# Paired heads in three attention stages of a fused block: score row halves side by side, values as the stationary operand in column halves, weights normalised before they are transposed

## The chip, the cores and the metric

One core of a Trainium2 chip runs the whole kernel. The metric is device time in microseconds (us). TensorE (PE) multiplies matrices; its weight loads are listed apart as PEld. VectorE is DVE, ScalarE is ACT, GpSimd is POOL, SyncE is SP. A matmul whose operands are plain float32 is issued as two instructions, one whose operands are float32r (the rounded high or low half of a split) as one.

## The reference

The reference is two transformer layers followed by a second block, on 512 tokens of width 1024. Three of its parts matter here.

- `swa_sinks`: 16 query heads of width 64 over 4 key heads. Query block n of 128 tokens sees key blocks n-1 and n, masked to a window of 128; a per-head sink joins the softmax.

```
s = einsum('bnqkgd,bnskd->bnkgqs', q, kb) * 64 ** -0.5        # banded: [128, 256] a block
p = softmax(concatenate([where(valid, s, -1e30), sink], -1))[..., :-1]
o = einsum('bnkgqs,bnskd->bnqkgd', p, vb)
```

- `stick_breaking_attention`: 8 heads of width 64 over all earlier keys.

```
z = einsum('bhqd,bhkd->bhqk', qb, k) * scale
log_one_minus = where(strict, log_sigmoid(-z), 0)
suffix = cumsum(log_one_minus, reverse) - log_one_minus
w = where(strict, exp(log_sigmoid(z) + suffix), 0);  o = w @ v
```

- `latent_attention`: 8 heads, keys of width 96, values of width 64, causal softmax.

## The kernel before

Tiles are 128 partitions by up to 512 columns. Weights arrive by DMA, are split by ACT and DVE into float32r halves (`weights`, lines 146 to 155), and every dense product is three float32r matmuls (`mm3` and `mmhl`, lines 157 to 166). The program is emitted in source order, and the framework's scheduler then orders each engine's instructions; each engine executes its own list strictly in that order.

**Banded stage** (`attention`, lines 1291 to 1500). Work goes by head pairs t = 0 to 7; a pair's two heads r sit in partitions 0 to 63 and 64 to 127 of the query tile `q`/`qhl` and of the key tile `kf`/`khl`. `proj(t)` makes the queries (24 matmuls `psq`). `scores(t)` (line 1383) writes score tiles `sc` in PSUM, head by head, three matmuls of 64 rows a block (line 1401; one float32 matmul for block 0, line 1397), and DVE masks each block and takes its row maximum (line 1402). `expo(t)` takes exponentials on ACT with their sums (line 1418), adds the sink and takes the reciprocal `den` on DVE (lines 1420, 1421). `mixed(t)` transposes the weights 128 by 128 into `pt` (line 1433), copies them out as `pT`, multiplies with `pT` stationary and the 64 value columns moving into `po` (line 1443), scales by `den` on DVE (line 1446) and transposes the result back (`pto`, line 1450). The loop over t weaves `scores(t-1)`, `proj(t)`, `mixed(t-2)` and `expo(t-1)`.

**Stick-breaking stage** (`second`, lines 1752 to 1790). Per head, `part1` makes the logits `z` (four float32 matmuls of 64 rows, line 1756, each followed by a mask matmul with `idr`, line 1757), then absolute value, exponential and logarithm on ACT, then three DVE passes (lines 1764 to 1766) for the halves `hl`. `part2` adds the triangular sums into `z` (20 matmuls, line 1774), takes the exponential (line 1776) and multiplies with the values stationary into 64 columns (line 1780). The loop keeps one head in flight: `part1(h)`, then `part2(h-1)`.

**Latent stage** (lines 1795 to 1921). `scores(h)` (line 1864), then `mixed(h)` a head later: exponentials, transposes (line 1880), copies `pT`, products with `pT` stationary into `po` (line 1887); after each second head one scaling by `den` (line 1916), four transposes `pto` (line 1919) and one copy `ob` (line 1920).

**Filler.** `fill(n)` (line 1661) issues n steps of the gate projection, three float32r matmuls `psg` of 512 columns each; 192 steps in all, and `fill(1000)` at the end of the latent stage issues what is left.

Of the kernel before, what the change touches and what calls it, by code (L numbers as in the profile page):

```python
# [1290 lines left out]
def attention(N, kvd, rd, gpost, after_half):  # L1291
# [3 lines left out]
    with ExitStack() as es:  # L1295
# [4 lines left out]
        with ExitStack() as e2:  # L1300
# [82 lines left out]
            def scores(t):  # L1383
                a = t // 4
                q, qhl = qs.pop(t)
                S = [[N.mp.tile([P, 2 * W], F32, tag="m", name="S") for _ in range(2)] for _ in range(4)]
                m = qp.tile([P, 4, 2], F32, tag="m", name="m")
                for j in range(4):
                    r = j % 2
                    rows = slice(64 * r, 64 * r + 64)  # L1390
                    ps = scp.tile([P, 2, 2 * W], F32, tag="sc", name="sc")
                    for n in (j - r, j - r + 1):
                        s0 = W if n == 0 else 0
                        qb = slice(n * W, (n + 1) * W)
                        pn = ps[:, n % 2, :]
                        if n == 0:
                            nc.tensor.matmul(pn[:, W:], lhsT=q[rows, qb], rhs=kf[rows, a, 0:W], start=True, stop=True, skip_group_check=True)
                        else:
                            kb = slice((n - 1) * W, (n + 1) * W)
                            for x, y, st, sp in ((0, 0, n == 2, False), (0, 1, False, False), (1, 0, False, True)):  # L1400
                                nc.tensor.matmul(pn, lhsT=qhl[rows, x, qb], rhs=khl[a][rows, y, kb], start=st, stop=sp, skip_group_check=True)
                        nc.vector.tensor_tensor_reduce(out=S[n][r][:, s0:], in0=pn[:, s0:], in1=mask[:, s0:], scale=1.0, scalar=-3e38, op0=ALU.add, op1=ALU.max, accum_out=m[:, n, r:r + 1])
                    yield
                sk = N.rows[:, None, 256 + 2 * t:258 + 2 * t].to_broadcast([P, 4, 2])
                nc.vector.tensor_tensor(out=m, in0=m, in1=sk, op=ALU.max)
                es_ = qp.tile([P, 4, 2], F32, tag="es", name="es")
                nc.vector.tensor_tensor(out=es_, in0=sk, in1=m, op=ALU.subtract)
                nc.vector.tensor_scalar(out=m, in0=m, scalar1=-1.0, scalar2=None, op0=ALU.mult)
                nc.scalar.activation(out=es_, in_=es_, func=AF.Exp)
                Ss[t] = S, m, es_  # L1410

            def expo(t):
# [6 lines left out]
                    yield  # L1419
                nc.vector.tensor_tensor(out=den, in0=den, in1=es_, op=ALU.add)  # L1420
                nc.vector.reciprocal(out=den, in_=den)
                Ss[t] = S, den

            def mixed(t):
                a = t // 4
                S, den = Ss.pop(t)
                po = N.mm.tile([P, 4, 2, 64], F32, tag="mm", name="po")
                for n in range(4):
                    s0 = W if n == 0 else 0
                    pt = scp.tile([P, 2, 2 * W], F32, tag="sc", name="pt")  # L1430
# [9 lines left out]
                    for r in range(2):  # L1440
                        d0 = (2 * a + r) * 64
                        for sb in range(s0 // W, 2):
                            nc.tensor.matmul(po[:, n, r, :], lhsT=pT[:, r, sb * W:(sb + 1) * W], rhs=v[:, n - 1 + sb, d0:d0 + 64], start=n == 0 and r == 0, stop=sb == 1, skip_group_check=True)  # L1443
                    yield
                ot = qp.tile([P, 4, 2, 64], F32, tag="ot", name="ot")
                nc.vector.tensor_tensor(out=ot, in0=po, in1=den[:, :, :, None].to_broadcast([P, 4, 2, 64]), op=ALU.mult)
                yield
                pt = N.mm.tile([P, T], F32, tag="mm", name="pto")
                for n in range(4):
# [160 lines left out]
def second(N, out, angd, hs):  # L1610
# [116 lines left out]
    with ExitStack() as e1:  # L1727
# [21 lines left out]

            return t[:, BASE[i] + P * max(0, q0 - i):BASE[i] + P * (4 - i)]  # L1750

        def part1(h):
            a, rows = h // 2, slice(64 * (h % 2), 64 * (h % 2) + 64)
            z = zp.tile([P, 1536], F32, tag="z", name="z")
            for i in range(4):
                nc.tensor.matmul(seg(z, i), lhsT=sk_[a][rows, i * P:(i + 1) * P], rhs=sq_[a][rows, i * P:], start=i < 3, stop=False, skip_group_check=True)  # L1756
                nc.tensor.matmul(z[:, BASE[i]:BASE[i] + P], lhsT=idr, rhs=msk, start=False, stop=False, skip_group_check=True)
# [9 lines left out]
            return z, hl, e  # L1767

        def part2(h, z, hl, w):
            rows = slice(64 * (h % 2), 64 * (h % 2) + 64)  # L1770
# [4 lines left out]
            fill(6)  # L1775
            nc.scalar.activation(out=w, in_=z[:, 0:1280], func=AF.Exp)
            fill(4)
            pv = N.mm.tile([P, T], F32, tag="mm", name="pv")
            for i in range(4):
                nc.tensor.matmul(pv[rows, i * P:], lhsT=sv[:, i, 64 * h:64 * h + 64], rhs=seg(w, i), start=i == 0, stop=i == 3, skip_group_check=True, tile_position=(0, 64 * (h % 2)))  # L1780
            nc.scalar.activation(out=oa[rows, h // 2, :], in_=pv[rows], func=AF.Copy)

        prev = None
        for h in range(9):
            cur = part1(h) if h < 8 else None
            fill(4)
# [9 lines left out]
    with ExitStack() as e1:  # L1796
# [71 lines left out]
                fill(1)  # L1868
            return S, mx

        def mixed(h, S, mx, po):
            sc = 96.0 ** -0.5
            r = h % 2
            nc.vector.tensor_scalar(out=mx, in0=mx, scalar1=-sc, scalar2=None, op0=ALU.mult)
            for i in range(4):
                nc.scalar.activation(out=S[i], in_=S[i], func=AF.Exp, scale=sc, bias=mx[:, i:i + 1], accum_out=den[:, i, r:r + 1])
                pt = ptp.tile([P, T], F32, tag="pt", name="pt")
                n = P * (i + 1)
                for sb in range(i + 1):
                    nc.tensor.transpose(pt[:, sb * P:(sb + 1) * P], S[i][:, sb * P:(sb + 1) * P], N.ident)  # L1880
                pT = tp.tile([P, T], F32, tag="pT", name="pT")
                if i % 2:
                    nc.vector.tensor_copy(pT[:, :n], pt[:, :n])
                else:
                    nc.scalar.activation(out=pT[:, :n], in_=pt[:, :n], func=AF.Copy)
                for sb in range(i + 1):
                    nc.tensor.matmul(po[:, i, r, :], lhsT=pT[:, sb * P:(sb + 1) * P], rhs=v[:, sb, 64 * h:64 * h + 64], start=i == 0 and r == 0 and sb == 0, stop=sb == i, skip_group_check=True)
                fill(1)

        heads(0)  # L1890
        wv = N.weights(N.ins["w_ukv"][1])
# [10 lines left out]
        for h in range(9):  # L1902
            if h < 8:
                if h % 2 == 0 and h < 6:
                    heads(h // 2 + 1)
                cur = scores(h)
            if prev is not None:
                g = h - 1
                if g % 2 == 0:
                    po = N.mm.tile([P, 4, 2, 64], F32, tag="mm", name="po")  # L1910
                    den = tp.tile([P, 4, 2], F32, tag="den", name="den")
                mixed(g, *prev, po)
                if g % 2:
                    nc.vector.reciprocal(out=den, in_=den)
                    ot = tp.tile([P, 4, 2, 64], F32, tag="x", name="ot", bufs=1)
                    nc.vector.tensor_tensor(out=ot, in0=po, in1=den[:, :, :, None].to_broadcast([P, 4, 2, 64]), op=ALU.mult)
                    pt = ptp.tile([P, T], F32, tag="pt", name="pto")
                    for n in range(4):
                        nc.tensor.transpose(pt[:, n * P:(n + 1) * P], ot[:, n].rearrange("p r d -> p (r d)"), N.ident)
                    nc.scalar.activation(out=ob[:, g // 2, :], in_=pt, func=AF.Copy)  # L1920
            prev = cur
    fill(1000)
    N.mmctx.close()
# [127 lines left out]
```

## Time and profile before

| what | us |
|---|---|
| median of 3 runs | 2767.73 (2764.96 to 2768.2) |
| the profiled execution, its own time | 2768.43 |
| span of that execution | 2766.7 |
| PE busy | 2680.9 (97% of the span) |
| PEld busy | 2330.6 (84%) |
| DVE busy | 1477.9 (53%) |
| ACT busy | 1167.9 (42%) |
| POOL busy | 27.4 (1%) |

The profile page gives shares over the whole span; the three stages of the change lie at 1716 to 1843 us (banded), 2369.8 to 2531 us (stick-breaking) and 2563 to 2664 us (latent). In a timeline the stretch of a merged row runs from its first start to its last end, and ends of matmuls are modelled, so the pace of PE is read from starts: (stretch - one duration) / (count - 1).

### The profile page before, as it was taken

The page shows a single profiled execution, that of the slowest core. Times are in us where ns is not written, and L with a number is a line of the kernel's source. Part 1 is how long each engine was busy: PE and PEld are TensorE (multiplying, and loading weights), DVE is VectorE, ACT ScalarE, POOL GpSimd, SP SyncE. Part 2 cuts the span into 40 slices and gives each one's busy share as a digit, 9 for nine tenths or more (in the row PEclk, how much of TensorE's full clock was granted, in tenths as well). Part 3 has the DMA queues.
Part 4 walks back from the last instruction along what each step waited for, and adds up shares of the span by engine and source line. Part 5 has one row for each costly group of instructions (what it writes and reads, how often), then busy time and mean ns, then how long its engine had stood idle before and what let it go on. Part 6 is the DMA issues. An engine that isn't in the chain of part 4 may idle for free.

```text
span 2766.7 us, 43687 instructions
## 1 busy us (share of the span) xinstructions
PE 2680.9 (97%) x17470; PEld 2330.6 (84%) x17470; DVE 1477.9 (53%) x2976; ACT 1167.9 (42%) x2072; POOL 27.4 (1%) x52
## 2 busy tenths in 40 slices
PE   8999988999999999999999999999999999999998
PEld 7888887788788999999888888888888898777877
DVE  8724466555557565467643447547424465234555
ACT  5223325345355554345432324445323335454643
POOL 0000000000000000000000000000000000000000
PEclk9999999999999999999999999899999999999999
DMA  6622316864765463245342323012222323113333
GB/s 212 218 94 98 115 63 203 238 174 129 214 209 142 133 215 109 96 138 180 115 133 92 99 92 141 25 38 93 98 94 97 114 85 115 61 61 105 115 126 99
DMA packets 207556, 344.20 MB, mean 124 GB/s; under 512 B 66164, under 2 KB 136180, under 8 KB 207352
## 3 DMA queue, kind: packets, MB, share of 16 engines
q1 hardware_dynamic: 206920, 341.13, 39.0%
q8 instruction: 137, 2.24, 0.3%
q14 instruction: 67, 0.55, 0.1%
q10 hardware_dynamic: 432, 0.28, 0.0%
HBM read 298.51 MB, written 41.26 MB: 123 GB/s over the span
## 4 chain that ended last, share of the span: by engine, by line
PE 88%; DVE 4%; DMA 3%; ACT 3%; issue 1%; SPq 0%; DVEq 0%; ACTq 0%
PE gu L165 11%; PE gu L164 11%; PE gu L166 11%; PE o L164 8%; PE o L166 8%; PE o L165 8%; PE ps L594 4%; PE ps L166 2%; PE ps L165 2%; PE ps L164 2%; PE psg L164 2%; PE psg L165 1%; PE psg L166 1%; PE po L1443 1%; PE z L1756 1%
## 5 line engine op out<-in xcount | busy, mean ns | idle before, releaser
L153 ACT ACTIVATE whl<-wr 128x1024 fp32r<-128x1024 f32 x417 | 439.3, 1059 | 729.3 <-PE gu L166 402.1
L154 DVE TENSOR_TENSOR whl<-wr,whl 128x1024 fp32r<-128x1024 f32 x417 | 508.1, 1222 | 374.1 <-ACT whl L153 373.0
L164 PE MATMUL gu<-xn,whl 128*128 128x512 f32 (+1 forms) x1200 | 436.7, 366 | 8.9 <-ACT xn L242 7.1
L165 PE MATMUL gu<-xn,whl 128*128 128x512 f32 (+1 forms) x1200 | 439.2, 366 | 3.9 <-DVE xn L243 3.9
L166 PE MATMUL gu<-xn,whl 128*128 128x512 f32 (+1 forms) x1200 | 438.0, 366 | 0.8 <-DVE whl L154 0.8
L166 PE MATMUL o<-a,whl 128*128 128x256 f32 (+1 forms) x906 | 297.7, 329 | 0.0
L165 PE MATMUL o<-a,whl 128*128 128x256 f32 (+1 forms) x906 | 296.8, 329 | 0.0
L164 PE MATMUL o<-a,whl 128*128 128x256 f32 (+1 forms) x906 | 296.3, 329 | 0.0
L164 PEld LDWEIGHTS gu<-xn,whl 128*128 128x128 f32 x1200 | 226.6, 190 | 45.1 <-ACT xn L242 7.3
L165 PEld LDWEIGHTS gu<-xn,whl 128*128 128x128 f32 x1200 | 228.0, 190 | 40.8 <-DVE xn L243 5.2
L166 PEld LDWEIGHTS gu<-xn,whl 128*128 128x128 f32 x1200 | 228.0, 190 | 37.0 <-DVE whl L154 1.2
L165 PE MATMUL gu<-pair,whl 128*128 128x256 f32 x704 | 200.2, 285 | 1.1 <-DVE pair L243 1.1
L166 PE MATMUL gu<-pair,whl 128*128 128x256 f32 x704 | 199.1, 283 | 1.2 <-DVE whl L154 1.2
L164 PE MATMUL gu<-pair,whl 128*128 128x256 f32 x704 | 199.2, 284 | 0.0
L165 PEld LDWEIGHTS o<-a,whl 128*128 128x128 f32 x906 | 170.7, 189 | 17.1
L166 PEld LDWEIGHTS o<-a,whl 128*128 128x128 f32 x906 | 170.6, 189 | 17.0
L164 PEld LDWEIGHTS o<-a,whl 128*128 128x128 f32 x906 | 170.3, 189 | 17.1
L594 PE MATMUL ps<-mxe,wraw 128*128 128x256 f32 x544 | 144.4, 416 | 15.2 <-DVE mxe L609 7.5
L594 PEld LDWEIGHTS ps<-mxe,wraw 128*128 128x128 f32 x544 | 108.9, 208 | 38.1 <-DVE mxe L609 7.7
L166 PEld LDWEIGHTS gu<-pair,whl 128*128 128x128 f32 x704 | 133.6, 190 | 2.0 <-DVE whl L154 1.4
L165 PEld LDWEIGHTS gu<-pair,whl 128*128 128x128 f32 x704 | 133.2, 189 | 2.4 <-DVE pair L243 1.7
L164 PEld LDWEIGHTS gu<-pair,whl 128*128 128x128 f32 x704 | 132.8, 189 | 1.0
(440 smaller groups left out, 4768.5 us busy)
## 6 DMA issues: line engine op xcount, KB each, us to landing
wr<-in_ffn_w_in_dram SPq DMA_DIRECT2D x204, 512.0 KB, 3.5
wr<-in_ffn_w_out_dram SPq DMA_DIRECT2D x99, 512.0 KB, 3.4
wr<-in_w_in_dram SPq DMA_DIRECT2D x38, 512.0 KB, 3.5
wraw<-in_w_rkvo_dram SPq DMA_DIRECT2D x32, 512.0 KB, 4.1
wr<-in_w_rkvo_dram SPq DMA_DIRECT2D x32, 512.0 KB, 4.6
wr<-in_w_ada_dram SPq DMA_DIRECT2D x24, 512.0 KB, 4.1
wr<-in_w_qo_dram SPq DMA_DIRECT2D x16, 512.0 KB, 3.4
gates<-xf SPq DMA_DIRECT2D x48, 128.0 KB, 1.8
```

The costliest lines, as they stand in the source:

```text
L153: nc.scalar.activation(out=hl[:, 0, :cols], in_=raw[:, :cols], func=AF.Copy)
L154: nc.vector.tensor_tensor(out=hl[:, 1, :cols], in0=raw[:, :cols], in1=hl[:, 0, :cols].bitcast(F32), op=ALU.subtract)
L164: nc.tensor.matmul(ps, lhsT=wh, rhs=xh, start=start, stop=False, **k)
L165: nc.tensor.matmul(ps, lhsT=wh, rhs=xl, start=False, stop=False, **k)
L166: nc.tensor.matmul(ps, lhsT=wl, rhs=xh, start=False, stop=stop, **k)
L594: nc.tensor.matmul(ps, lhsT=w[:, b * P:(b + 1) * P], rhs=x, start=start, stop=stop)
L1443: nc.tensor.matmul(po[:, n, r, :], lhsT=pT[:, r, sb * W:(sb + 1) * W], rhs=v[:, n - 1 + sb, d0:d0 + 64], start=n == 0 and r == 0, stop=sb ...
L1756: nc.tensor.matmul(seg(z, i), lhsT=sk_[a][rows, i * P:(i + 1) * P], rhs=sq_[a][rows, i * P:], start=i < 3, stop=False, skip_group_check=True)
```

## The change

Banded stage: `scores` now emits the two heads of a pair alternately, matmul by matmul. `expo` is followed by eight `tensor_scalar` instructions on POOL that multiply the exponentials by `den` in place. `mixed` makes the 64 value columns the stationary operand, writes head r to partitions 64r to 64r+63 of `po` (`tile_position=(0, 64 * r)`), alternates the heads, and splits `po` directly: the scaling on DVE and the four transposes `pto` are gone.

Stick-breaking stage: heads go by pairs. `products` emits the logits of both heads alternately and then all mask matmuls; `logs` is the ACT and DVE chain of one head; `weigh` the triangular sums and the exponential; `mixed` alternates the two heads' column halves of one `pv` tile. The loop runs over pairs, with 18 fill steps in each.

Latent stage: `weigh` normalises on POOL (four instructions a head) and copies the transposes into a layout by key block; `mixed` multiplies a pair at once, values stationary, column halves alternating; the scaling, the `pto` transposes and two of the float32 tiles are gone.

```diff
             def scores(t):
...
-                for j in range(4):
-                    r = j % 2
-                    for n in (j - r, j - r + 1):
-                            for x, y, st, sp in ((0, 0, n == 2, False), (0, 1, False, False), (1, 0, False, True)):
-                                nc.tensor.matmul(pn, lhsT=qhl[rows, x, qb], rhs=khl[a][rows, y, kb], start=st, stop=sp, skip_group_check=True)
+                for n2 in range(0, 4, 2):
+                    pss = [scp.tile([P, 2, 2 * W], F32, tag="sc", name="sc") for _ in range(2)]
+                    for n in (n2, n2 + 1):
+                        for x, y, st, sp in ((0, 0, n == 2, False), (0, 1, False, False), (1, 0, False, True)) if n else ((None, None, True, True),):
+                            for r in range(2):
+                                if n:
+                                    nc.tensor.matmul(pn, lhsT=qhl[rows, x, qb], rhs=khl[a][rows, y, kb], start=st, stop=sp, skip_group_check=True)
...
-                Ss[t] = S, den
+                for n in range(4):
+                    for r in range(2):
+                        nc.gpsimd.tensor_scalar(out=S[n][r][:, s0:], in0=S[n][r][:, s0:], scalar1=den[:, n, r:r + 1], scalar2=None, op0=ALU.mult)
+                Ss[t] = S
             def mixed(t):
...
-                            nc.tensor.matmul(po[:, n, r, :], lhsT=pT[:, r, sb * W:(sb + 1) * W], rhs=v[:, n - 1 + sb, d0:d0 + 64], start=n == 0 and r == 0, stop=sb == 1, skip_group_check=True)
+                    for sb in range(s0 // W, 2):
+                        for r in range(2):
+                            nc.tensor.matmul(po[64 * r:64 * r + 64, n * W:(n + 1) * W], lhsT=v[:, n - 1 + sb, d0:d0 + 64], rhs=pT[:, r, sb * W:(sb + 1) * W], start=n == 0, stop=sb == 1, skip_group_check=True, tile_position=(0, 64 * r))
-                nc.vector.tensor_tensor(out=ot, in0=po, in1=den[:, :, :, None].to_broadcast([P, 4, 2, 64]), op=ALU.mult)
-                    nc.tensor.transpose(pt[:, n * W:(n + 1) * W], ot[:, n].rearrange("p r d -> p (r d)"), N.ident)
-                N.split(pt, o, 0, T)
+                N.split(po, o, 0, T)
...
+        def products(a):
+            zs = [zp.tile([P, 1536], F32, tag="z", name="z") for _ in range(2)]
             for i in range(4):
+                for r, z in enumerate(zs):
+                    nc.tensor.matmul(seg(z, i), lhsT=sk_[a][rows, i * P:(i + 1) * P], rhs=sq_[a][rows, i * P:], start=i < 3, stop=False, skip_group_check=True)
+            for z in zs:
+                for i in range(4):
+                    nc.tensor.matmul(z[:, BASE[i]:BASE[i] + P], lhsT=idr, rhs=msk, start=False, stop=False, skip_group_check=True)
...
-        for h in range(9):
-            cur = part1(h) if h < 8 else None
-            fill(4)
-            if prev is not None:
-                part2(h - 1, *prev)
-            prev = cur
+        zs, ws = products(0), None
+        for a in range(4):
+            if ws:
+                mixed(a - 1, ws)
+            hls, ws = zip(*(logs(z) for z in zs))
+            fill(10)
+            weigh(zs[0], hls[0], ws[0])
+            fill(5)
+            weigh(zs[1], hls[1], ws[1])
+            fill(3)
+            if a < 3:
+                zs = products(a + 1)
+        fill(2)
+        mixed(3, ws)
...
+        def weigh(S, mx, pT):
+                nc.vector.reciprocal(out=den[:, i:i + 1], in_=den[:, i:i + 1])
+                nc.gpsimd.tensor_scalar(out=S[i], in0=S[i], scalar1=den[:, i:i + 1], scalar2=None, op0=ALU.mult)
...
+        def mixed(a, pTs):
+            po = N.mm.tile([P, T], F32, tag="mm", name="po")
+            for sb in range(4):
+                for r, pT in enumerate(pTs):
+                    nc.tensor.matmul(po[64 * r:64 * r + 64, sb * P:], lhsT=v[:, sb, 64 * h:64 * h + 64], rhs=pT[:, sb, sb:].rearrange("p i q -> p (i q)"), start=sb == 0, stop=sb == 3, skip_group_check=True, tile_position=(0, 64 * r))
+            nc.scalar.activation(out=ob[:, a, :], in_=po, func=AF.Copy)
```

The scheduler does not keep the alternation everywhere. Engine PE, banded stage, the scores of the second head pair; two `sc` tiles with consecutive numbers are the two heads of one block pair, so a row with a count is one head on its own. Before:

```order
L1397 MATMUL sc_16833<-kf_16343,q0_16803 128x128
L1401 MATMUL sc_16739<-khl0_16344,qhl_16717 128x256 x3
L1401 MATMUL sc_16843<-khl0_16344,qhl_16805 128x256 x3
L1401 MATMUL sc_16749<-khl0_16344,qhl_16717 128x256 x3
L1401 MATMUL sc_16855<-khl0_16344,qhl_16805 128x256 x3
```

and with the change, with the first products behind them:

```order
L1402 MATMUL sc_16825<-kf_16343,q0_16811 128x128
L1400 MATMUL sc_16825<-khl0_16344,qhl_16813 128x256 x3
L1402 MATMUL sc_16826<-kf_16343,q0_16811 128x128
L1400 MATMUL sc_16826<-khl0_16344,qhl_16813 128x256 x3
L1400 MATMUL sc_16851<-khl0_16344,qhl_16813 128x256 x6
L1400 MATMUL sc_16852<-khl0_16344,qhl_16813 128x256 x6
L1442 MATMUL pt_16881<-ident_72,S_16720 128x128
L1442 MATMUL pt_16881<-ident_72,S_16721 128x128
L1452 MATMUL po_16880<-pT_16884,v_16346 64x128 x2
```

This pair runs head by head; the scores of the first pair alternate. The `po` row holds one matmul of each head, next to each other, and so do all 28 groups of `po` rows.

Engine PE, stick-breaking stage, the logits `z` of one head (`sq`, `sk` are its queries and keys, `msk` and `idr` the mask) and the products `pv`. Before:

```order
L1756 MATMUL z_22341<-sq1_21226,sk1_21230 128x512
L1757 MATMUL z_22341<-msk_22177,idr_22178 128x128
L1756 MATMUL z_22341<-sq1_21226,sk1_21230 128x384
L1757 MATMUL z_22341<-msk_22177,idr_22178 128x128
L1756 MATMUL z_22341<-sq1_21226,sk1_21230 128x256
L1757 MATMUL z_22341<-msk_22177,idr_22178 128x128
L1780 MATMUL pv_22335<-e_22203,sv_21233 64x512
```

and with the change, second pair (`e_22220` and `e_22229` are the two heads' weights):

```order
L1761 MATMUL z_22365<-sq1_21234,sk1_21238 128x512
L1761 MATMUL z_22365<-sq1_21234,sk1_21238 128x384
L1761 MATMUL z_22365<-sq1_21234,sk1_21238 128x256
L1761 MATMUL z_22365<-sq1_21234,sk1_21238 128x128
L1764 MATMUL z_22365<-msk_22185,idr_22186 128x128 x4
L1791 MATMUL pv_22382<-e_22229,sv_21241 64x512
L1791 MATMUL pv_22382<-e_22220,sv_21241 64x384
L1791 MATMUL pv_22382<-e_22229,sv_21241 64x384
L1791 MATMUL pv_22382<-e_22220,sv_21241 64x256
L1791 MATMUL pv_22382<-e_22229,sv_21241 64x256
```

The mask matmuls no longer stand between the logits. The logits alternate between heads in the first pair only; `pv` alternates but for its first matmul, which stands apart.

Engine ACT, stick-breaking stage, third pair with the change (L1769 absolute value, L1770 exponential, L1771 logarithm, L1784 the weights, L1792 the result of the pair before):

```order
L1769 ACTIVATE e<-z 128x1280
L1792 ACTIVATE oa<-pv 128x512
L1769 ACTIVATE e<-z 128x1280
L1770 ACTIVATE e<-e 128x1280 x2
L1771 ACT_TABLE_LOAD
L1771 ACTIVATE e<-e 128x1280 x2
L153 ACTIVATE whl<-wr 128x1024
L1784 ACT_TABLE_LOAD
L1784 ACTIVATE e<-z 128x1280 x2
```

Both heads of a pair now pass through each function together, with the copy of the pair before ahead of the second head.

## Rows read from the trace of the kernel before

**Rows 1.** The page, part 1.
```profile
PE 2680.9 (97%) x17470; PEld 2330.6 (84%) x17470; DVE 1477.9 (53%) x2976; ACT 1167.9 (42%) x2072; POOL 27.4 (1%) x52
```
**Rows 2.** Windows: stretch, length, busy us (count) by engine, granted clock, DMA share, GB/s.
```profile
1716.00:1745.40 29.40, 25.30 (x112) 20.64 (x110) 12.86 (x56) 12.99 (x41) 0.00 (x0) 0.59 0.06 19
...
2369.80:2531.00 161.20, 160.26 (x682) 113.86 (x681) 57.89 (x69) 82.25 (x73) 0.29 (x1) 0.97 0.21 68
```
**Rows 3.** Timeline, banded stage: start, stretch, engine, line; filler, transposes, products.
```profile
1743.97 0.78 PE L164 MATMUL psq<-xn,whl 128*128 128x512 f32 x1
...
1750.09 0.93 PE L1433 MATMUL pt<-ident,S 128*128 128x128 f32 x7
...
1752.88 1.10 PE L1443 MATMUL po<-v,pT 128*128 128x64 f32 x8
```
**Rows 4.** Timeline, gate projection: the first and the sixteenth of consecutive starts.
```profile
2384.16 0.39 PE L164 MATMUL psg<-xn,whl 128*128 128x512 f32 x1
...
2387.56 0.40 PE L164 MATMUL psg<-xn,whl 128*128 128x512 f32 x1
```
**Rows 5.** Timeline, time-mixing stage, line 1088: alternating row halves, 64 rows each.
```profile
538.62 1.23 PE L1088 MATMUL sc<-ar,kb 64*128 64x128 f32 x16 [0.47 <-DVE ar L1077]
```
**Rows 6.** Timeline, time-mixing stage: lines 1216 and 1226 on different column halves.
```profile
628.08 0.22 PE L1226 MATMUL st<-vsa,kt 128*64 128x64 f32 x1
628.09 0.22 PE L1216 MATMUL xy<-vsa,S 128*64 128x64 f32 x1
628.14 0.22 PE L1226 MATMUL st<-vsa,kt 128*64 128x64 f32 x1
628.14 0.22 PE L1216 MATMUL xy<-vsa,S 128*64 128x64 f32 x1
628.20 0.63 PE L1226 MATMUL st<-vsa,kt 128*64 128x64 f32 x9
```
**Rows 7.** Timeline, stick-breaking stage: logits, masks and products of one head.
```profile
2396.36 1.12 PE L1756 MATMUL z<-sq,sk 64*128 64x512 f32 x2
2397.42 0.33 PE L1757 MATMUL z<-msk,idr 128*128 128x128 f32 x1
2397.67 0.91 PE L1756 MATMUL z<-sq,sk 64*128 64x384 f32 x2
...
2399.65 2.37 PE L1780 MATMUL pv<-e,sv 128*64 128x512 f32 x8
2401.95 0.49 PE L1756 MATMUL z<-sq,sk 64*128 64x128 f32 x2
...
2402.53 0.44 PE L166 MATMUL psg<-xn,whl 128*128 128x512 f32 x1
```
**Rows 8.** Groups by form, 2369 to 2531 us: the stick-breaking chain on ACT and DVE.
```profile
L1761 ACT ACT_TABLE_LOAD x8 | 10.3, 1283 | 0.1
L1760 ACT ACTIVATE e<-e 128x1280 f32<-128x1280 f32 x8 | 10.2, 1275 | 0.2
...
L1781 ACT ACTIVATE oa<-pv 64x512 f32<-64x512 f32 x8 | 4.7, 592 | 51.5 <-PE pv L1780 51.5
...
L1764 DVE SCALAR_TENSOR_TENSOR sp<-z,e 128x1280 f32<-128x1280 f32 x8 | 11.9, 1492 | 79.4 <-ACT e L1761 79.4
...
L1765 DVE CAST hl<-sp 128x1280 fp32r<-128x1280 f32 x8 | 6.6, 824 | 0.2
```
**Rows 9.** Groups by form, banded stage: exponentials and reciprocal.
```profile
L1418 ACT ACTIVATE S<-S,m 128x256 f32<-128x256 f32 x48 | 23.6, 493 | 0.0
...
L1421 DVE RECIPROCAL den<-den 128x8 f32<-128x8 f32 x8 | 1.6, 202 | 0.2
```
**Rows 10.** Groups by form, POOL, whole span.
```profile
L1198 POOL TENSOR_TENSOR sp<-S,pcol 64x256 f32<-64x256 f32 x24 | 16.2, 677 | 32.7 <-DVE S L1233 25.8 <-DVE mv L1250 5.6
...
L1019 POOL TENSOR_SCALAR_AFFINE_SELECT eye<-ones 64x256 f32<-64x256 f32 x1 | 0.5, 499 | 385.0 <-PE o L166 385.0
```
**Rows 11.** Groups by form, 2563 to 2672 us: transposes of the latent stage.
```profile
L1880 PE MATMUL pt<-ident,S 128*128 128x128 f32 x80 | 14.9, 293 | 2.6 <-ACT ob L1920 2.6
```

More of the change, by code (lines that the diff above doesn't have):

```diff
@@ L1402, in scores @@
-                        nc.vector.tensor_tensor_reduce(out=S[n][r][:, s0:], in0=pn[:, s0:], in1=mask[:, s0:], scale=1.0, scalar=-3e38, op0=ALU.add, op1=ALU.max, accum_out=m[:, n, r:r + 1])
-                    yield
+                        kb = slice((n - 1) * W, (n + 1) * W)
+                        for x, y, st, sp in ((0, 0, n == 2, False), (0, 1, False, False), (1, 0, False, True)) if n else ((None, None, True, True),):
+                            for r in range(2):
+                                rows = slice(64 * r, 64 * r + 64)
+                                pn = pss[r][:, n % 2, :]
+                                if n:
+                                    nc.tensor.matmul(pn, lhsT=qhl[rows, x, qb], rhs=khl[a][rows, y, kb], start=st, stop=sp, skip_group_check=True)
+                                else:
+                                    nc.tensor.matmul(pn[:, W:], lhsT=q[rows, qb], rhs=kf[rows, a, 0:W], start=True, stop=True, skip_group_check=True)
@@ L1404, in scores @@
+                    for n in (n2, n2 + 1):
+                        s0 = W if n == 0 else 0
+                        for r in range(2):
+                            nc.vector.tensor_tensor_reduce(out=S[n][r][:, s0:], in0=pss[r][:, n % 2, s0:], in1=mask[:, s0:], scale=1.0, scalar=-3e38, op0=ALU.add, op1=ALU.max, accum_out=m[:, n, r:r + 1])
+                        yield
                 sk = N.rows[:, None, 256 + 2 * t:258 + 2 * t].to_broadcast([P, 4, 2])
@@ L1766, in part1, with weigh @@
             nc.vector.tensor_tensor(out=hl[:, 1], in0=sp, in1=hl[:, 0].bitcast(F32), op=ALU.subtract)
-            return z, hl, e
-        def part2(h, z, hl, w):
-            rows = slice(64 * (h % 2), 64 * (h % 2) + 64)
+            return hl, e
+        def weigh(z, hl, w):
             for x in range(2):
@@ L1774, in part2, with mixed @@
                         nc.tensor.matmul(seg(z, i, j), lhsT=ntri if j == i else none, rhs=seg(hl[:, x], j), start=False, stop=x == 1 and j == 3, skip_group_check=True)
-            fill(6)
             nc.scalar.activation(out=w, in_=z[:, 0:1280], func=AF.Exp)
-            fill(4)
+        def mixed(a, ws):
             pv = N.mm.tile([P, T], F32, tag="mm", name="pv")
             for i in range(4):
-                nc.tensor.matmul(pv[rows, i * P:], lhsT=sv[:, i, 64 * h:64 * h + 64], rhs=seg(w, i), start=i == 0, stop=i == 3, skip_group_check=True, tile_position=(0, 64 * (h % 2)))
-            nc.scalar.activation(out=oa[rows, h // 2, :], in_=pv[rows], func=AF.Copy)
-        prev = None
-        for h in range(9):
-            cur = part1(h) if h < 8 else None
-            fill(4)
-            if prev is not None:
-                part2(h - 1, *prev)
-            prev = cur
+                for r, w in enumerate(ws):
+                    h = 2 * a + r
+                    nc.tensor.matmul(pv[64 * r:64 * r + 64, i * P:], lhsT=sv[:, i, 64 * h:64 * h + 64], rhs=seg(w, i), start=i == 0, stop=i == 3, skip_group_check=True, tile_position=(0, 64 * r))
+            nc.scalar.activation(out=oa[:, a, :], in_=pv, func=AF.Copy)
+        zs, ws = products(0), None
[12 more added lines that the diff above has]
+        mixed(3, ws)
     eB.close()
@@ L1879, in mixed @@
                 for sb in range(i + 1):
-                    nc.tensor.transpose(pt[:, sb * P:(sb + 1) * P], S[i][:, sb * P:(sb + 1) * P], N.ident)
-                pT = tp.tile([P, T], F32, tag="pT", name="pT")
+                    nc.tensor.transpose(pt[:, sb], S[i][:, sb * P:(sb + 1) * P], N.ident)
                 if i % 2:
-                    nc.vector.tensor_copy(pT[:, :n], pt[:, :n])
+                    nc.vector.tensor_copy(pT[:, 0:i + 1, i], pt[:, 0:i + 1])
                 else:
-                    nc.scalar.activation(out=pT[:, :n], in_=pt[:, :n], func=AF.Copy)
@@ L1886, in mixed @@
-                for sb in range(i + 1):
-                    nc.tensor.matmul(po[:, i, r, :], lhsT=pT[:, sb * P:(sb + 1) * P], rhs=v[:, sb, 64 * h:64 * h + 64], start=i == 0 and r == 0 and sb == 0, stop=sb == i, skip_group_check=True)
+                    nc.scalar.activation(out=pT[:, 0:i + 1, i], in_=pt[:, 0:i + 1], func=AF.Copy)
                 fill(1)
+        def mixed(a, pTs):
+            po = N.mm.tile([P, T], F32, tag="mm", name="po")
+            for sb in range(4):
+                for r, pT in enumerate(pTs):
+                    h = 2 * a + r
+                    nc.tensor.matmul(po[64 * r:64 * r + 64, sb * P:], lhsT=v[:, sb, 64 * h:64 * h + 64], rhs=pT[:, sb, sb:].rearrange("p i q -> p (i q)"), start=sb == 0, stop=sb == 3, skip_group_check=True, tile_position=(0, 64 * r))
+            nc.scalar.activation(out=ob[:, a, :], in_=po, func=AF.Copy)
@@ L1909, in second @@
                 if g % 2 == 0:
-                    po = N.mm.tile([P, 4, 2, 64], F32, tag="mm", name="po")
-                    den = tp.tile([P, 4, 2], F32, tag="den", name="den")
-                mixed(g, *prev, po)
+                    pTs = [tp.tile([P, 4, 4, P], F32, tag=f"pT{r}", name="pT", bufs=1) for r in range(2)]
+                weigh(*prev, pTs[g % 2])
                 if g % 2:
[L1914 to L1920, printed above, removed]
+                    mixed(g // 2, pTs)
             prev = cur
```

37 lines of the change are left out of this document (11 added, 26 removed).

## The prediction

> **What bounds the kernel now.** I began with the busy times of the engines: PE is busy for 97% of the span, DVE for 53%, ACT for 42%, POOL for 1% [rows 1]. Then the windows of the stages: in the stick-breaking one PE is busy for 160.26 of 161.20 us [rows 2], so the stage is as long as its stream of matmuls, and an instruction less on PE is time won, while ACT and DVE have half of the stage in hand. The banded stage is the exception: in its first 29.40 us the granted clock is 0.59 and PE idles for 4.1 us [rows 2]. The timelines then give the pace of each kind of matmul, from starts, and the groups give the lengths of the other engines' steps, which tell whether a chain still hides behind matmuls.
>
> **Prices on PE.** Eight products `po` take (1.10 - 0.275)/7 = 0.118 us each, 0.275 being one alone; seven transposes (0.93 - 0.273)/6 = 0.110 [rows 3]. A `psg` of 512 columns takes (2387.56 - 2384.16)/15 = 0.227 [rows 4]. Alternating row halves go faster: (1.23 - 0.27)/15 = 0.064 [rows 5] for 128 columns, for which transposes need 0.110. Alternating column halves start within 0.01 us of each other and every pair needs some 0.06, where nine on one side need (0.63 - 0.22)/8 = 0.051 each [rows 6]; so two cost little more than one. I count a pair of neighbours on different halves as one.
>
> **Banded stage.** Before, 112 products are 224 instructions: 224 x 0.118 = 26.4 us. Now there are again 112 matmuls, 224 instructions, in 28 groups that alternate strictly: 112 slots, and one more at each entry, (112 + 28) x 0.115 = 16.1, a price between those of rows 3. That gives -10.3. The 32 transposes `pto` go: -32 x 0.110 = -3.5. The order has 57 neighbours of different row halves among the scores instead of 28: -29 x 0.115 = -3.3, at the price of rows 3 since a score matmul streams 256 columns in one pass. Against it stand 16 more changes between whole tiles and halves. Their price shows in the logits: Z of 512 columns takes 2397.42 - 2396.36 = 1.06 until the mask starts, while its share of the eight products, 2401.95 - 2399.65 = 2.30 for 1280 columns, would be 0.92; and the mask takes 0.25 until the next Z, where a transpose of that size takes 0.11 [rows 3, 7]. Both give 0.14, and I take 0.15: +2.4. The stream gets 14.7 shorter. DVE's scaling goes from beside PE and counts nothing.
>
> The clock: 29.40 us at 0.59 instead of 1 cost 12.1 [rows 2]. The clock is at 1.2 GHz until the run of fillers that begins at 1743.97 [rows 3]. With the change a run of 16 `psq` stands just behind the first transposes, so the stretch should be shorter. I take -5; at least 0, and at most -10, nearly all that the stretch costs.
>
> New waits: the first transpose of a pair now waits for the reciprocal and POOL too. POOL has no such operation before; the nearest are one input over 256 columns, 0.499, and two inputs, 0.677 [rows 10]. Reciprocal 0.20 [rows 9], as much for the addition, and two operations on POOL at 0.5 make 1.4 a pair, 11.2 in eight pairs; if scores and fillers cover all, 0. I take +5, bounds 0 and +12, since some pairs have fillers ahead of their first transpose. The Trainium skill ("GPSIMD Engine Reference", 3.1 Elementwise and 1. Specifications) gives 1.03 cycles per element at 1.2 GHz for a body with so few operations, which by an estimate is 0.22 us for 256 columns; no row of this case shows such an operation at 128 partitions. By it the wait would be about half, and the whole 2 us less.
>
> **Stick-breaking stage.** Z and its masks take (2399.65 - 2396.36) + (2402.53 - 2401.95) = 3.87 a head [rows 7]. Without masks in between a head is 2.30, four masks of some 0.06 and one change of 0.1, 2.65: six heads save 6 x 1.22 = 7.3. In the first pair the heads alternate: 7.74 becomes 2.30 and eight masks with their changes, 3.0, and saves 4.7. The products of a pair, one alone and then seven that alternate, take 1.06 for the first, 2.30 for the rest and 0.1, or 3.46 instead of 2 x 2.30: four pairs save 4.6. In sum -16.6.
>
> What comes late: both heads' chains are now started together, and the fillers that cover them fell from 116 steps to 74 in this stage by the order. In the third pair, from the end of Z, there stand V (2.4), oa (0.59), an absolute value (1.27), two exponentials (2.55), a table load (1.28), a logarithm (1.27), DVE's 1.49 and 0.82: 11.7 us until the triangular matmuls may start [rows 8]. Its cover is V and 24 `psg`, 2.4 + 24 x 0.227 = 7.9, so PE waits 3.8. In the first pair the chain is two absolute values, a load, and the same from there, 11.2, against 41 `psg` and masks, 9.8: 1.4. For the second heads I add 1.2 a pair, one step of ACT: +10 in all. Bounds: 0 if tables and exponentials go in better time, +16 if the other two pairs wait as the third.
>
> **Latent stage.** Before, 160 instructions x 0.118 = 18.9; now four pairs of the same shape as the stick-breaking products, 4 x 3.46 = 13.8: -5.1. Sixteen transposes less, -1.8. The transposes that wait 2.6 us for `ob` [rows 11] no longer have that copy behind a transpose: -2. POOL's four operations a head have a whole head's scores as cover, so nothing. The 56 filler matmuls that are now left at the end move there and are not more in number; they count nothing.
>
> **The sum.** -14.7 - 5 + 5 - 16.6 + 10 - 8.9 = -30.2, against the profiled execution's 2768.43: **2738**. The median of the runs lies 0.7 lower, which the rounding takes in.
>
> **Rivals.**
> *A, column halves don't overlap.* Then banded products cost 224 slots instead of 140 (+9.7), the V's +4.6, the latent ones +4.6: 2757. The starts 0.01 apart [rows 6] speak against it; but there 64 columns move, here 128 to 512, with a new weight for each. The Trainium skill ("TensorE: Matmul & The Clock Gate", Part 3: Packing small matmuls, The mechanism) lets a weight load overlap running matmuls only when the row group differs, and both column halves here use all rows. The trace speaks against that rule for 64 moving columns; no run here shows it for longer ones. Chance 0.06.
>
> *B, slower: POOL sets the pace of the banded stage.* The transposes of a pair now need all exponentials, 8 x 0.493 = 3.9 at most, the reciprocal 0.2 and two POOL operations at 0.677, 1.4: 5.5 us [rows 9, 10], where before a transpose needed one exponential. All eight operations at 0.677 are 5.4, the same. Uncovered in eight pairs that is 44: without my +5, 2733 + 44 = **2777**. The gain is gone from a wait of 4.4 us a pair, and from 5.1 the kernel is slower by over 0.2%. For it: PE idled already 4.1 us at the stage's start [rows 2]. Against: scores of the next pair and 24 `psq` (24 x 0.227 = 5.4) stand between. Chance 0.09.
>
> *C, the stick-breaking pairs hang on ACT and DVE.* If every pair waits 3.8 as the third, and each second head another DVE chain of 3.8 (1.49 + 0.82 + 1.49), that is 30 instead of 10: 2758, and 2752 to 2765 as half or more of that is covered. Against: half of ACT and DVE is free [rows 2]. Chance 0.10.
>
> *D, the clock stays at 1.2 GHz for longer.* Shorter, sparser PE work in the banded stage could keep the low clock for 30 us more, which costs 15: 2753. Chance 0.05. That the change doesn't do what it says holds in part already, since the order leaves heads unmixed in three of four pairs of logits, and is in the sum.
>
> **How the numbers follow.** The forecast has 0.70. Its own range: 2718 with the clock's best (-5 more) and no new waits (-5 and -10); 2756 with the waits at their upper bounds (+7, +6) and no gain by the clock (+5). The range of **2718 to 2760** takes in A, D and half of C. What a measurement of this kernel can tell from no change is 0.2%, 5.5 us, so faster means below 2762. Faster: 0.70 + 0.06 + 0.05 + some 0.04 of C = **0.85**; same: the rest of C, **0.06**; slower: B, **0.09**.
>
> **What would show it.** Right: `po` pairs starting together and 28 groups of some 0.6 us; `pv` of a pair near 3.5; no `pto`; waits of triangular matmuls for DVE's halves of about 4 us in the third pair and near 1 elsewhere; a low clock of 10 to 15 us at the banded stage's start. Wrong: `po` rows at 0.118 an instruction (A), transposes that wait for POOL in each pair (B), the triangular matmuls late in all pairs (C), a window at 0.6 for over 40 us (D).

## The result and the profile after

The changed kernel takes 2735.91 us (median of 4 runs, 2732.79 to 2740.61) where the kernel before takes 2767.97 beside it: ratio 0.9883, 95% interval 0.9861 to 0.9905. The forecast was 2738, with a range of 2718 to 2760. Run again later, beside three of its variants, the change stood at 0.9903 (0.9888 to 0.9918).

The page of the changed kernel, part 1, answers to [rows 1]. The windows have the columns of [rows 2]: the same 29.40 us as there (the banded stage begins 5.6 us later here), the stretch with the low clock in it, and the two other stages:

```profile
PE 2638.4 (96%) x17326; PEld 2288.5 (84%) x17326; DVE 1472.2 (54%) x2992; ACT 1154.1 (42%) x2061; POOL 118.6 (4%) x148
```
```profile
1716.00:1745.40 29.40, 19.24 (x98) 14.68 (x98) 13.61 (x52) 13.50 (x45) 10.41 (x13) 0.77 0.16 54
1729.60:1743.30 13.70, 7.03 (x19) 4.97 (x20) 2.43 (x14) 7.85 (x34) 8.31 (x11) 0.50 0.01 1
2360.78:2485.69 124.91, 115.92 (x561) 88.89 (x561) 48.65 (x55) 61.44 (x54) 0.30 (x1) 0.97 0.21 65
2485.69:2633.30 147.61, 143.75 (x683) 112.11 (x683) 81.08 (x200) 79.42 (x154) 35.38 (x32) 0.99 0.39 126
```

PE now idles 9.0 us in the stick-breaking stage (124.91 - 115.92), where it idled 0.9 before. Since filler steps moved from one stage to the next, the stages are compared without them: a stage's length in the timeline less 0.227 us [rows 4] for each `psg` in it.

| stretch, us | before | after |
|---|---|---|
| banded: from transposes `pr` to the last product `o` | 176.3 | 164.0 |
| stick-breaking: first logits to first `rot`, less 360 or 240 `psg` | 84.5 | 75.7 |
| latent: first `rot` to first `ps<-br`, less 216 or 336 `psg` | 78.6 | 66.0 |

So the stages gave -12.3, -8.8 and -12.6, 33.7 in all, in one execution of each kernel. The experiments below hold more executions of the same stages, before and with the change: banded 176.3 to 178.0 and 163.0 to 164.0, stick-breaking 81.5 to 84.5 and 75.7 to 80.4, latent 78.4 to 80.9 and 64.4 to 68.6. So tenths in the accounts below belong to these two executions, and the gain of the stick-breaking stage is known to a few us only. What lies outside the stages moves too: the unchanged stretch up to `pr` took between 1696 and 1709 us in the 14 profiled executions of this study.

The timeline of the changed kernel at the first banded pair, columns as in [rows 3], with the wait and its releaser at the end of a row, and a later group of products:

```profile
1735.65 1.06 PE L1442 MATMUL pt<-ident,S 128*128 128x128 f32 x2 [7.95 <-POOL S L1429]
1737.22 0.70 PE L1452 MATMUL po<-pT,v 128*64 128x128 f32 x4 [0.52 <-DVE pT L1447]
...
1750.30 0.66 PE L1452 MATMUL po<-pT,v 128*64 128x128 f32 x8
```

and in the stick-breaking stage, logits and masks of the first pair, then its products around those of a head of the second pair, then the longest wait, in the third:

```profile
2360.78 2.43 PE L1761 MATMUL z<-sq,sk 64*128 64x512 f32 x16 [0.69 <-ACT sv L1718]
2363.14 1.11 PE L1764 MATMUL z<-msk,idr 128*128 128x128 f32 x8
...
2387.29 1.07 PE L1791 MATMUL pv<-e,sv 128*64 128x512 f32 x2
2389.88 2.42 PE L1761 MATMUL z<-sq,sk 64*128 64x512 f32 x8
2392.23 0.66 PE L1764 MATMUL z<-msk,idr 128*128 128x128 f32 x4
2392.82 2.37 PE L1791 MATMUL pv<-e,sv 128*64 128x512 f32 x14
...
2441.32 0.79 PE L1783 MATMUL z<-hl,ntri 128*128 128x512 f32 x1 [4.43 <-DVE hl L1775]
```

Sixteen logit instructions that alternate (the first pair) take as long, 2.36 us by starts, as eight of one head, 2.35; a group of eight `po` takes 0.59 until the next start, a change of tiling included, where eight at the 0.118 of [rows 3] would take 0.94. Of the first pair's products the first stands apart (2387.29, 1.00 until the next start); the `pv` in the order shown ahead of the prediction are these too, beside the second pair's logits.

### The profile page after: what moved, and what is told of

It is laid out like the page before. It is cut to its first block, busy times and chain, and to the rows that moved or that the text cites. A ratio compares the mean times of both kernels' runs of the same rounds, so it can differ in the third digit from the quotient of the medians.

```text
span 2735.0 us, 43654 instructions
## 1 busy us (share of the span) xinstructions
PE 2638.4 (96%) x17326; PEld 2288.5 (84%) x17326; DVE 1472.2 (54%) x2992; ACT 1154.1 (42%) x2061; POOL 118.6 (4%) x148
## 4 chain that ended last, share of the span: by engine, by line
PE 85%; DVE 5%; DMA 4%; issue 3%; ACT 3%; SPq 0%; POOL 0%; DVEq 0%; ACTq 0%; POOLq 0%
PE gu L164 12%; PE gu L165 12%; PE gu L166 12%; PE o L164 8%; PE o L166 8%; PE o L165 8%; PE ps L594 4%; PE ps L164 2%; PE ps L166 2%; PE ps L165 2%; PE psg L164 1%; PE psg L166 1%; PE psg L165 1%; PE z L1783 1%; DMA kk<-kk 1%
```

## The experiments

Ratios are to the kernel before, run beside each.

**One part alone.** Three kernels each take the change of one function only: `attention`, or the stick-breaking or the latent part of `second`.

> Banded part of the change alone. Theory (the three parts add up, each worth what its stretch of the trace lost): the stretch from the first psq of the stage to the first psg-like product of the output projection went down by about 13 us, so 2768 - 13 = 2755 us, ratio 0.995. Rival (the shared fillers and the clock tie the parts together, so that the banded part alone gives little): 2763 to 2770. A first transpose that waits some 8 us for POOL and a low clock of about 14 us are expected by both.

> Stick-breaking part alone. Theory: 16 fewer changes of tiling and alternating products are worth some 20 us of PE, waits for DVE's halves give back 9, so -11 net: 2757 us, ratio 0.996. Rival (the waits for ACT and DVE eat the gain, and what the stretch lost are only fillers that moved to the latent stage): within 3 us of the kernel before, 2765 to 2771.

> Latent part alone. Theory: 160 short products become 32 long ones in alternating halves (-5), 16 transposes (-2) and the idle time around ob and ot (about 4) go: -10, 2758 us, ratio 0.9965. Rival (without the fillers that the stick-breaking part leaves over, the stage has no cover and POOL's chain of 0.6 to 1.7 us an operation shows): -3 or less, 2765 and above.

Banded alone: 0.9959 (0.9948 to 0.9971). Stick-breaking alone: 0.9966 (0.9954 to 0.9977). Latent alone: 0.9953 (0.9937 to 0.9969). Of 2771.5 these are -11, -9 and -13 us, and the rival of each expectation falls. The sum, -34, agrees with the 32 of the whole within the intervals: the parts add. POOL's longer operations in the latent stage cost it nothing even with the filler of the kernel before.

**Products head by head**, in all three stages, to take away the neighbours on different column halves:

```diff
-            for i in range(4):
-                for r, w in enumerate(ws):
+            for r, w in enumerate(ws):
+                for i in range(4):
                     h = 2 * a + r
```
(and the like in the two other `mixed`).

> The whole change, but the two heads' products stand one head after the other in all three stages, so that neighbours on different column halves are left only at the border between heads. Theory (neighbouring column halves overlap, and that is where the products' gain is from): up to 10 us in the banded stage and 4.6 in each of the others come back: 2736 + 15 to 19 = 2751 to 2755 us. Rival A of the prediction (column halves do not overlap; the gain is that of fewer changes and longer streams): within 3 us of the change, 2733 to 2739.

0.9863 (0.9848 to 0.9879), 2733.81 us: no slower than the change. That is the time of rival A's line and not of the theory's. But the time alone misleads here, and the rows of the products say what one head after the other costs; timeline, stick-breaking stage, the products of the two heads of one pair:

```profile
2388.65 2.37 PE L1791 MATMUL pv<-e,sv 128*64 128x512 f32 x8
...
2394.55 2.37 PE L1791 MATMUL pv<-e,sv 128*64 128x512 f32 x8
```

Each head takes 2.30 us by starts, 4.60 a pair; with the change a pair takes 1.00 for the lone first matmul and 2.30 for the rest, 3.30. Column halves overlap: rival A is false for 128 to 512 moving columns as well, and its time came about for another reason. In the latent stage the loss shows (72.3 us without fillers, against 66.0). In the stick-breaking stage it is won back and more: 69.4 against 75.7. The groups of PE, the triangular matmuls and the products, of the change and of this kernel, with the idle time ahead of them last:

```profile
L1783 PE MATMUL z<-hl,ntri 128*128 128x512 f32 (+1 forms) x64 | 22.2, 389 | 7.6 <-DVE hl L1775 7.6
L1791 PE MATMUL pv<-e,sv 128*64 128x256 f32 (+3 forms) x64 | 13.8, 442 | 1.4 <-ACT e L1784 1.4
```
```profile
L1783 PE MATMUL z<-hl,ntri 128*128 128x512 f32 (+1 forms) x64 | 20.6, 356 | 0.5 <-DVE hl L1776 0.3 <-DVE hl L1775 0.2
L1791 PE MATMUL pv<-e,sv 128*64 128x256 f32 (+3 forms) x64 | 18.1, 439 | 0.0
```

The products cost 4.3 us more of busy time and the waits of 9.0 shrink to 0.5. In the banded stage nothing moved (164.0 both): the order still holds 36 neighbours on different halves, of 84 with the change, and groups in the order 0 0 1 1 also took 0.59 us, their instructions starting in twos 0.01 us apart, as in the change. So this run says nothing of banded products that are really in series.

**Why the triangular sums wait.** ACT's first step of a pair writes into `e`, of which there are two buffers, and the products of the pair before still read them. The changed kernel's answer for that line, and that of a kernel with four buffers:

```profile
its engine sat idle before it (us, times) until:
  PE pv L1791: 24.0, 3
```
```profile
its engine sat idle before it (us, times) until:
  PE z L1764: 13.6, 5
```
```diff
-            e = tp.tile([P, 1280], F32, tag="e", name="e")
+            e = tp.tile([P, 1280], F32, tag="e", name="e", bufs=4)
```

> The whole change with four buffers instead of two for the tile e, so that the absolute values of a pair no longer have to wait until the products of the pair before have read their weights (ACT waits 24.0 us there in the changed kernel). Theory (PE's waits for DVE's halves, 7.6 us, and the low clock behind the longest come from that chain standing behind the products): the waits shrink to 2 us or less, 2736 - 6 to 9 = 2727 to 2730 us. Rival (ACT's and DVE's work of a pair is itself as long as its cover, and the order brings the triangular sums forward by as much as the chain): waits stay at 6 us or more, 2733 to 2739.

0.9853 (0.9833 to 0.9874), 2727.16 us; the stage without fillers 65.8 instead of 75.7, and the triangular matmuls wait 1.6:

```profile
L1783 PE MATMUL z<-hl,ntri 128*128 128x512 f32 (+1 forms) x64 | 20.6, 356 | 1.6 <-DVE hl L1775 1.6
```

The chain no longer stands behind the products. Two other ways to the same end, more cover and products in series in this stage alone:

```diff
-            fill(10)
+            fill(13)
             weigh(zs[0], hls[0], ws[0])
-            fill(5)
+            fill(6)
             weigh(zs[1], hls[1], ws[1])
```

> The whole change with fill(13) and fill(6) instead of fill(10) and fill(5), so that 16 more filler steps stand in the stick-breaking stage and 16 fewer at the end of the latent one. Theory (the waits lack cover): 12 more psg matmuls a pair are 2.7 us of cover; the waits of 4.4, 1.6 and 1.4 us go down to 2 us in all, 2736 - 5 = 2731 us. Rival (the order puts the added fillers where nothing waits): 2734 to 2739, waits in all as before.

> The whole change, but the stick-breaking products stand one head after the other. Theory (overlapping column halves shorten these products, from 4.60 us a pair to 3.30, but alternating ties the chain of the next pair to both heads' weights): the products cost 5 us more, and waits of 7 to 9 us and the low clock go: 2729 to 2734 us. Rival (the gain of the run with all products in series came from the latent stage): 2738 to 2742.

The fillers: 0.9866 (0.9845 to 0.9887), waits for DVE's halves 1.6 us as expected, though the products now wait 2.7 for `e` instead of 1.4; stage 69.2, and 2.5 of the gain go back in the latent stage (68.5), which lost that cover. The products in series: 0.986 (0.9839 to 0.988), waits 2.4 us, stage 71.3. By the stage both theories hold, since the change left as it is took 75.7 to 80.4 there, and giving up the overlap pays as long as the buffers are two. By the totals none of these three runs is told from the change: each interval overlaps its 0.9861 to 0.9905.

A part of what they win is the clock's. In the change it is at 1.2 GHz from 2439.6 to 2446.4 us, behind the wait of 4.43; PE is busy for 5.1 of these, and half of that, some 2.5 us, is what it costs. In these three runs, and in the one with all products in series, it stays at 2.4 GHz from the first logits to the last products.

**The first banded pair.** Is the wait of 7.95 us POOL's? The eight normalisations on DVE instead (`nc.vector.tensor_scalar`):

> The whole change with the banded weights normalised on DVE instead of POOL. Theory (the long wait of the first pair, 8 us, is the chain of maxima and eight exponentials, not POOL, whose part of it is the 0.7 us of one operation; later pairs have cover): between -3 and +4 us, 2733 to 2740. Rival B of the prediction in what is left of it (POOL's operations of 0.68 and 0.97 us, 56 us of the stage's 124, hold transposes up): 2730 or less.

0.9883 (0.9858 to 0.9908), as the change. DVE takes 0.348 us for what POOL takes 0.968, and the first transpose still waits 7.50 (the order of the whole stage is another, so only this wait is compared):

```profile
1728.72 1.15 PE L1442 MATMUL pt<-ident,S 128*128 128x128 f32 x4 [7.50 <-DVE S L1429]
```

So POOL isn't the bound of this wait. Then each block normalised as soon as its own exponentials are there:

```diff
                     for r in range(2):
                         nc.scalar.activation(out=S[n][r][:, s0:], ..., accum_out=den[:, n, r:r + 1])
                     yield
-                nc.vector.tensor_tensor(out=den, in0=den, in1=es_, op=ALU.add)
-                nc.vector.reciprocal(out=den, in_=den)
-                for n in range(4):
-                    s0 = W if n == 0 else 0
+                    nc.vector.tensor_tensor(out=den[:, n], in0=den[:, n], in1=es_[:, n], op=ALU.add)
+                    nc.vector.reciprocal(out=den[:, n], in_=den[:, n])
                     for r in range(2):
                         nc.gpsimd.tensor_scalar(...)
```

The unaltered change, this kernel and the next two ran on one chip.

> The change itself, unaltered, beside the three runs below on one chip: 0.988 of the kernel before, 2733 to 2740 us where that takes 2768.

> The whole change, but each block's two weights are normalised as soon as their own two exponentials are done, not after all eight. Theory (the 8 us wait of the first pair is the chain of maxima, eight exponentials, reciprocal and one operation of POOL; six exponentials of 0.4 to 0.5 us stand in it that need not): the wait goes down by about 2.5 us to 5.5, 2.5 us off the change. Rival (the wait is DVE's and ACT's work on the second pair that stands ahead, or POOL): wait within 1 us of 8, no change.

Control 0.9903 (0.9888 to 0.9918), 2736.91 us; block by block 0.9889 (0.9874 to 0.9903), 2733.93. The wait falls to 4.64 and the stage to 160.4, against 163.0 in the control:

```profile
1731.32 1.05 PE L1440 MATMUL pt<-ident,S 128*128 128x128 f32 x2 [4.64 <-POOL S L1427]
```

The intervals of the two totals overlap; the wait itself went by 3.3, so the six exponentials behind the first two were the larger part of what can go.

> Four buffers for e and normalisation block by block together. Theory (the two waits are in different stages and add): 8 to 10 us from the buffers and 2.5 from the blocks, 0.984 of the kernel before, 2723 to 2727 us where the change takes 2736. Rival (the stretches trade): no better than the buffers alone, 0.9853.

0.9851 (0.9827 to 0.9875), 2723.31 us: the fastest here, and 13.6 us below the control beside it. No triangular matmul waits in it, and the stage without fillers takes 63.6. Against the buffers alone (0.9853, on another chip) the gain of the blocks can't be told.

**The scores.** Emitted head by head (`for r in range(2)` ahead of the loop over x and y):

> The whole change, but the banded scores of the two heads are emitted one head after the other; in the order 118 neighbouring score matmuls are on different row halves instead of 145, and 116 before the change. Theory (the term S of the prediction, 0.115 us for each such neighbour): 27 x 0.115 = 3 us more, 2739 us. Rival (the pace does not hang on neighbours, as PE starts matmuls of free halves a few places apart): within 1.5 us of the change, 2735 to 2737, and the length of the scores in the trace unchanged.

0.9886 (0.987 to 0.9903), 2733.67 us; the stage takes 164.3, against 163.0 and 164.0 in the two executions of the change. Groups of PE, the change and this kernel:

```profile
L1400 PE MATMUL sc<-khl,qhl 64*128 64x256 f32 x144 | 20.3, 300 | 0.1
```
```profile
L1400 PE MATMUL sc<-khl,qhl 64*128 64x256 f32 x144 | 20.6, 302 | 0.1
```

27 neighbours fewer are worth 0.3 us of busy time, not 3 (the three counts of the expectation hold 88 neighbours of the time-mixing stage besides, which has tiles of the same name). The rival's reason shows in the rows. Ten scores that alternate strictly, in the change, and eleven in the order 0 0 1 1 1 0 0 0 1 1 1, in this kernel:

```profile
1802.59 0.85 PE L1400 MATMUL sc<-khl,qhl 64*128 64x256 f32 x10
```
```profile
1802.47 0.97 PE L1400 MATMUL sc<-khl,qhl 64*128 64x256 f32 x11
```

They take 0.79 and 0.91 until the next start; eleven in series, at 0.115, would take 1.27. So PE starts a matmul of a free row half though it stands some places further on. In the whole stage 35 score instructions of this kernel start within 0.02 us of the score before, 33 with the change and 30 before it: the run took away neighbours, but no overlap.

## Why the prediction was right, step by step

The total came within some 2 us, and partly because errors cancelled: the stages were forecast at -14.7, -6.6 and -8.9, and gave -12.3, -8.8 and -12.6.

- **Banded products** (-10.3, +2.4 for changes, -3.5 for `pto`): right. Groups of eight take 0.59 and of four 0.37, that is 0.11 for each slot of two instructions and 0.15 to enter.
- **Scores alternating (-3.3)**: the reason failed. I priced 29 more neighbours in the order, but by starts only 3 more scores overlap, and 27 neighbours fewer changed next to nothing. The size is open. From each start to the next, without idle time and with half of the time at 1.2 GHz taken off, the scores took an estimated 24.4 us before and 21.9 with the change. They also stand in 24 unbroken rows instead of 33, which may be the cause; no run tests it. The whole stream, by the stage less what clock and waits did (next two points), gave -12.3 + 7.3 - 7.1 = -12.1, against -14.7.
- **Clock (-5)**: right in kind. The stretch at 1.2 GHz went from 23.9 us in the records (1721.5 to 1745.4) to 13.7, where rival D had it longer, and PE was busy for only 7.03 of those. Half of the busy time is what it costs: 3.5 now and 10.8 before (21.6 busy), -7.3.
- **New waits in the banded stage (+5)**: PE idles 14.8 us of the stage instead of 7.7, +7.1, and not where I put it. I spread 1.4 us of reciprocal and POOL over eight pairs; one wait of 7.95 in the first pair is the most of it, later pairs are covered, and 1.3 are the last products `o`, which now wait for their weights. It is the chain that rival B named (all exponentials before the first transpose), once instead of eight times, and without POOL as its cause.
- **POOL's price** was outside my bounds: 0.968 us for 256 columns, where I took 0.5 and at most 0.677. It didn't matter: of POOL's 56 us in the stage's 124 only the first operation holds PE up for long.
- **Logits (-12.0)**: -10.0. The first pair takes 2.36 + 0.94 = 3.30, each of the six other heads 2.35 + 0.59 = 2.94: 20.9 in all, against 8 x 3.87 = 31.0. Mis-sized were the masks: four take 0.59, not 0.35.
- **Products of the stick-breaking stage (-4.6)**: 4 x (4.60 - 3.30) = -5.2, right.
- **Waits there (+10)**: 9.0 in all, 4.43 in the third pair against 3.8, 1.38 in the first against 1.4. The mechanism I gave, a chain counted from the end of the products, is right, and the buffers of `e` are why it starts there; I hadn't named them. Rival C is false: the second heads wait 0.19 and 1.61, the last products 1.38.
- **The clock in that stage** I had left out. Logits, products and waits (9.0 less the 0.9 of before) make -7.1 of the -8.8. Before, 10.2 us of the stage lay at 1.2 GHz with PE busy throughout, with the change 6.8 with 5.1 busy: some -2.6 by the same halving. That is 0.9 more in sum than was measured, which stays open. Where such stretches fall differs between executions of one program, so this part is luck.
- **Latent (-8.9)**: -12.6. The products gave -4.9 (from 18.1, by starts and without idle time, to 4 x 3.30) and the transposes -1.8 as priced. Mis-sized was the idle time around `ob` and `ot`: I counted the 2.6 of [rows 11] and overlooked the rows of the transposes back and their like. Groups of the kernel before, 2531 to 2672 us, then of the change:

```profile
L1887 PE MATMUL po<-lv,pT 128*128 128x64 f32 x160 | 21.8, 275 | 0.4 <-ACT pT L1885 0.2 <-DVE pT L1883 0.2
...
L1919 PE MATMUL pto<-ident,ot 128*128 128x128 f32 x16 | 2.7, 295 | 2.2 <-DVE ot L1916 2.2
```
```profile
L1901 PE MATMUL pt<-ident,S 128*128 128x128 f32 x80 | 12.8, 275 | 0.9 <-ACT pT L1905 0.9
```

2.6 + 0.4 + 2.2 = 5.2 us idle became 0.9: -4.3 instead of -2. These make -11.0; one stretch of 3.4 us at 1.2 GHz in the records instead of two is worth up to 1.7 more.

The three stages gave -33.7, against -30.2. Left open: products that are in series in the banded stage, and logits that alternate in the later pairs of the stick-breaking stage, where the order keeps the heads apart; neither was tried.

## What to carry to other kernels

Pairing heads on the two halves of the array shortens PE's stream by what the starts of paired matmuls promise, but it also ties one pair's buffers to both heads: look which tile the next pair's first step writes, and give it a buffer, or the gain turns into a wait. A normalisation moved ahead of a transpose costs the length of the chain up to it once, at the stage's start, where nothing covers it; make that chain as short as one block. And a price for a wait should be put into the one place in the order where cover is missing, not spread over all. Overlap of array halves is to be counted by starts in a trace, not by neighbours in the order.

## What the runs showed of the hardware

- POOL is slower than its nearest rows before. Groups by form of the changed kernel:

```profile
L1429 POOL TENSOR_SCALAR S<-S,den 128x256 f32<-128x256 f32 x48 | 45.4, 968 | 0.0
...
L1897 POOL TENSOR_SCALAR S<-S,den 128x512 f32<-128x512 f32 x8 | 13.7, 1714 | 0.0
...
L1897 POOL TENSOR_SCALAR S<-S,den 128x256 f32<-128x256 f32 x8 | 7.4, 926 | 0.4 <-DVE den L1896 0.4
L1897 POOL TENSOR_SCALAR S<-S,den 128x128 f32<-128x128 f32 x8 | 4.8, 606 | 84.1 <-DVE den L1896 76.4 <-PE psg L166 7.8
```

  In the latent stage it multiplies by a column in 0.606 us for 128 columns, 0.926 for 256 and 1.714 for 512, (1714 - 606) / 384 = 2.9 ns for each added column. The estimate by the Trainium skill ("GPSIMD Engine Reference", 3.1 Elementwise) was 0.22 us for 256; the measured 0.93 to 0.97 is over four times that, and decides.
- PE overlaps column halves though both use all rows: 3.30 us for a pair of `pv` against 4.60. The rule cited at rival A (the Trainium skill, "TensorE: Matmul & The Clock Gate", Part 3: Packing small matmuls, The mechanism), that a weight load overlaps running matmuls only when the row group differs, does not hold here. Neighbours in the order need not be on different halves: banded groups in the order 0 0 1 1 take the 0.59 us of 0 1 0 1, and eleven scores in the order 0 0 1 1 1 0 0 0 1 1 1 take 0.91 where a series would take 1.27.
- A wait can cost twice. In the change the clock was at 1.2 GHz behind the wait of 4.43 us: three triangular matmuls took 0.64 us by starts there, and 0.34 after 2446.4.

```profile
2444.47 0.84 PE L1783 MATMUL z<-hl,none 128*128 128x384 f32 x3
...
2446.77 0.51 PE L1783 MATMUL z<-hl,none 128*128 128x384 f32 x3
```

  The control is the same program, with the same wait of 1.61 us in the second pair, but there the clock was at 1.2 GHz behind that one too: the next eight logits took 4.27 us by starts instead of 2.35, and the stage 80.4 instead of 75.7 without fillers. In the change the wait of 1.61 was followed by no such stretch, so it is not the wait alone that decides.

```profile
2407.74 0.50 PE L1783 MATMUL z<-hl,ntri 128*128 128x512 f32 x1 [1.61 <-DVE hl L1775]
...
2409.27 4.33 PE L1761 MATMUL z<-sq,sk 64*128 64x512 f32 x8
2413.54 1.11 PE L1764 MATMUL z<-msk,idr 128*128 128x128 f32 x4
```
